# Memory normalised once inside the long plan; GLU and three key blocks as three fp32r products; six key and value blocks traced ahead of the GLU

## The chip, the cores and the metric

The kernel runs on one core of a Trainium2 chip. The metric is the device time of one execution in microseconds. The engines are named as the profile names them: PE is TensorE (matmuls; PEld its weight loads), DVE is VectorE, ACT is ScalarE, POOL is GpSimd, and SP is the engine whose queue issues nearly all transfers (SPq). Each engine works through its instructions in program order.

## The reference

A two-layer encoder trunk on 512 frames of 1024 channels with 256 memory tokens. Layer 0 projects the normalised input once and feeds two branches: an S5 state-space mixer with a GLU, and a convolution module; layer 1 is chunked attention. Each layer then cross-attends to the memory. The parts that the change touches:

```python
def s5_mixer(...):
    ...
    y = y.reshape(bsz, L, S5_WIDTH) + d_skip * uf
    z = jax.nn.gelu(y)
    out = z * jax.nn.sigmoid(z @ glu_w + glu_b)          # GLU: 512 x 512

def mem_cross_attention(h, mem_n, w_qg, w_kv, w_o):
    q, g = jnp.split(h @ w_qg, 2, axis=-1)
    k, v = jnp.split(mem_n @ w_kv, 2, axis=-1)           # 1024 x 2048, in both layers
    ...
    return (o * jax.nn.silu(g)) @ w_o

def reference(...):
    mem_n = rms_norm(mem, mem_norm_g)
    for layer in range(DEPTH):
        x = x + (ssm_conv_layer if layer % 2 == 0 else chunk_attention_layer)(...)
        x = x + mem_cross_attention(rms_norm(x, xa_norm_g[layer]), mem_n, ...)
    return rms_norm(x, final_norm_g)
```

## The kernel before, in words

All activations lie transposed: 128 channels on the partitions, tokens along the free axis, so x is eight tiles of 128x512 and the memory eight of 128x256. A matrix product in float32 is made of three products of rounded operands (type fp32r): each operand is split into a rounded part "hi" and the rest "lo", and hi·hi, hi·lo and lo·hi are added up in PSUM (mm3, proj). A weight block of 512 KB is loaded into one of three buffers "raw", ACT rounds it into "whi" (two buffers), and POOL, or DVE where the call says so, subtracts to get "wlo" (three buffers); this is weights(), and split() does the same for activations. A few products use the float32 operands as they are (native): the GLU's four blocks (line 923), key blocks 0 to 2 of layer 0 (NATIVE, line 704; the branch of line 664), and the S5, convolution and broadcast products.

Layer 0 is one long plan (PLAN, line 705): u, z, c and g are blocks of the input projection, v steps of the convolution's taps (two loads "cw" each), a, b and o the preparation, the scan and the output of one S5 slice of four, m and n the memory's statistics, l and s the LayerNorm of the convolution. m loads the eight memory tiles into two buffers "mt", squares them on ACT and adds them up on POOL; n makes the reciprocal root. After the plan come the GELU of the S5 outputs (zs), the memory's normalisation (mem_norm, line 631), which loads the memory again tile by tile, makes a float32 copy in "uu" and its hi and lo parts in "og", then the four GLU blocks, the LayerNorm's application, and the twelve key and value blocks of layer 0 in the order KVORDER, and the output projection w_out. A key block is 24 matmuls of 256 columns as three products, a value block 48 (token_major). In layer 1 mem_norm (line 1377) loads and normalises the memory a third time.

What the text gives is the traced order. Between the start of the plan and the first cross-attention PE's instructions are not pinned to it: a scheduler sorts each engine's instructions by readiness and priority when the program is built, and code under tc.high_priority() goes first. On the chip the resulting order of each engine is fixed. A buffer of a tag is handed out again when its last reader has finished, so an instruction or a load that writes a new tile may wait for that.

## Time and profile before

| | |
|---|---|
| median of 3 runs | 988.85 us (988.27 to 993.58) |
| profiled execution | 992.0 us, span 990.1 us |
| PE busy | 958.3 us (97%) |
| PEld busy | 820.5 us (83%) |
| DVE, ACT, POOL busy | 561.1, 468.8, 441.3 us |
| DMA | 113.72 MB, mean 115 GB/s |

The span goes from the first to the last instruction of the profiled execution. Busy time of PE is modelled from the starts of the matmuls; a native float32 matmul shows as two records. The granted clock is given as a share of full speed, so 0.50 is 1.2 GHz.

### The profile page before, as it was taken

How to read it: one execution, taken by the hardware profiler on the slowest of the kernel's cores; microseconds unless marked ns; L12 is line 12 of the kernel's file. 1: busy time of each engine (PE TensorE's matmuls, PEld its weight loads, DVE VectorE, ACT ScalarE, POOL GpSimd, SP SyncE). 2: the span in 40 equal slices, each digit the busy share in tenths (PEclk: the TensorE clock that was granted, in tenths of full speed). 3: DMA queues.
4: the chain of work that ended last, by engine and by line, in shares of the span. 5: the costliest groups of instructions: out<-in, count | busy, mean ns of one | idle time of the engine just before them, and what ended most of it. 6: DMA issues, size and time to landing. Idle time of an engine off the chain costs nothing.

```text
span 990.1 us, 14347 instructions
## 1 busy us (share of the span) xinstructions
PE 958.3 (97%) x5336; PEld 820.5 (83%) x5336; DVE 561.1 (57%) x1372; ACT 468.8 (47%) x845; POOL 441.3 (45%) x245
## 2 busy tenths in 40 slices
PE   8999999989999999999999999999999999999996
PEld 7788898858888888888798887877888998888895
DVE  7975356766244334453568767688667313333476
ACT  6333445456443434344366655656545543333352
POOL 1022332129766334447645434444327983433241
PEclk9999997999999999999999999999999999999998
...
GB/s 292 119 194 177 196 160 170 113 127 234 192 85 107 65 85 64 84 75 107 65 96 75 75 67 94 75 75 75 65 43 139 156 185 107 64 86 79 50 169 108
DMA packets 53621, 113.72 MB, mean 115 GB/s; under 512 B 13232, under 2 KB 24624, under 8 KB 53552
## 3 DMA queue, kind: packets, MB, share of 16 engines
...
q8 instruction: 42, 0.69, 0.3%
q14 instruction: 27, 0.22, 0.1%
...
## 4 chain that ended last, share of the span: by engine, by line
PE 33%; DVE 10%; ACT 3%; issue 2%; POOL 1%; DMA 1%; POOLq 0%; DVEq 0%; ACTq 0%
PE ps_proj L81 27%; PE ps_att L81 2%; PE ps_tr L84 2%; DVE pe L158 2%; DVE ps_att L1275 1%; PE ps_acc L81 1%; DVE o L153 1%; ACT whi L173 1%; PE ps_tr L81 1%; DVE h L162 1%; ACT pe L1262 1%; POOL wlo L153 1%; DVE z L153 1%; DVE s L1274 1%; DVE qk L153 1%
## 5 line engine op out<-in xcount | busy, mean ns | idle before, releaser
L153 POOL TENSOR_TENSOR wlo<-raw,whi 128x1024 fp32r<-128x1024 f32 x130 | 317.2, 2444 | 406.6 <-ACT whi L173 360.1
L81 PE MATMUL ps_proj<-h,whi 128*128 128x512 f32 x1184 | 302.0, 399 | 2.4 <-DVE ang L153 2.4
L81 PEld LDWEIGHTS ps_proj<-h,whi 128*128 128x128 f32 x1184 | 218.9, 190 | 47.6 <-issue 5.1
L173 ACT CAST whi<-raw 128x1024 fp32r<-128x1024 f32 x148 | 155.3, 1050 | 197.7 <-PE ps_proj L81 97.2
L81 PE MATMUL ps_proj<-h,wlo 128*128 128x512 f32 x592 | 151.0, 393 | 0.0
L81 PE MATMUL ps_proj<-og,whi 128*128 128x512 f32 (+1 forms) x672 | 134.9, 347 | 0.5 <-DVE og L153 0.5
L81 PEld LDWEIGHTS ps_proj<-h,wlo 128*128 128x128 f32 x592 | 110.8, 189 | 22.6
L81 PEld LDWEIGHTS ps_proj<-og,whi 128*128 128x128 f32 x672 | 107.6, 188 | 18.0 <-DVE og L153 2.0
L81 PE MATMUL ps_proj<-og,wlo 128*128 128x512 f32 (+1 forms) x344 | 73.5, 348 | 0.1
L81 PEld LDWEIGHTS ps_proj<-og,wlo 128*128 128x128 f32 x344 | 56.1, 188 | 8.8 <-POOL wlo L153 0.4
L153 DVE TENSOR_TENSOR pt<-ps_tr,pt 128x512 fp32r<-128x512 f32 (+1 forms) x80 | 40.0, 527 | 34.8 <-ACT pt L173 34.7
L173 ACT CAST pt<-ps_tr 128x512 fp32r<-128x512 f32 (+1 forms) x80 | 34.2, 460 | 48.2 <-PE ps_tr L84 48.0
L1262 ACT ACTIVATE pe<-ps_att,s 128x128 f32<-128x128 f32 (+3 forms) x64 | 33.5, 525 | 37.7 <-DVE s L167 34.0
L158 DVE TENSOR_SCALAR_CACHE_REDUCE pe<-pe,s 128x256 f32<-128x256 f32 (+3 forms) x96 | 48.5, 522 | 1.8
L153 DVE TENSOR_TENSOR z<-ps_proj,rb 128x512 f32<-128x512 f32 x32 | 22.1, 690 | 45.4 <-PE ps_proj L81 45.3
L153 POOL TENSOR_TENSOR sa<-sa,sq 128x512 f32<-128x512 f32 (+1 forms) x28 | 39.0, 1394 | 18.7 <-ACT sq L233 18.3
L153 DVE TENSOR_TENSOR x<-ps_proj,x 128x512 f32<-128x512 f32 (+1 forms) x38 | 22.9, 603 | 41.5 <-PE ps_proj L81 41.5
L153 DVE TENSOR_TENSOR kv<-ps_proj,kv 128x256 fp32r<-128x256 f32 (+1 forms) x24 | 12.2, 510 | 60.2 <-ACT kv L173 59.3
L162 DVE SCALAR_TENSOR_TENSOR h<-x,par,h 128x512 fp32r<-128x512 f32 x24 | 38.5, 1612 | 13.5 <-ACT h L252 13.5
L81 PEld LDWEIGHTS ps_proj<-x,cw 128*128 128x128 f32 x320 | 41.9, 202 | 4.7 <-DMA cw<-in_cw_dram 2.4
L81 PE MATMUL ps_proj<-x,cw 128*128 128x64 f32 (+4 forms) x320 | 41.4, 281 | 2.3 <-DMA cw<-in_cw_dram 1.7
L84 PE MATMUL ps_tr<-ident,pe 128*128 128x128 f32 x224 | 34.2, 274 | 3.4 <-DVE pe L158 2.4
...
## 6 DMA issues: line engine op xcount, KB each, us to landing
...
```

The source lines that it names most:

```text
L81: return self.keep(nc.tensor.matmul(*args, **kw))
L84: return self.keep(nc.tensor.transpose(*args))
L153: (eng or V).tensor_tensor(out, a, b, op=op)
L158: V.tensor_scalar(out=out, in0=in0, scalar1=s, scalar2=None, op0=op, op1=ALU.add, accum_out=small(1))
L162: V.scalar_tensor_tensor(out=out, in0=a, scalar=s, in1=b, op0=op0, op1=op1)
L173: A.copy(hi, src)
L1262: A.activation(st_["pe"][i], ps[:, c:c + n], AF.Exp, bias=nb, accum_out=st_["sums"][:, i:i + 1])
L1274: V.reduce_max(init, ps[:, :nf], axis=AX.X)
L1275: V.tensor_tensor_reduce(out=ps[:, nf:n], in0=ps[:, nf:n], in1=st["tz"][:, MEM - (n - nf):], scale=1.0, scalar=init, op0=ALU.add, op1=ALU. ...
```

## The change

The memory tiles are loaded once for layer 0, in pairs, into the "x" buffers that the plan leaves free, squared from there, kept, and normalised in a new stage w of the plan between a3 and b3; n moves ahead of a3. Their hi parts go to "ev" tiles and their lo parts to one "uu" and three "x" tiles, without a float32 copy. NATIVE and the native branches are gone: the three key blocks and the GLU are three products like the rest, and the GLU's inputs are split on ACT and DVE. In layer 0 the weight splits of the key and value blocks alternate between DVE and POOL. Six of these blocks are traced before the GLU (KVFIRST), the other six stay behind it. Outputs that had "ev" tiles of their own overwrite "sq", "gate" and "uu" tiles. In layer 1 the memory is loaded in four pairs into "kv" buffers.

```diff
@@ -120,7 +120,7 @@
     sm = ctx.enter_context(tc.tile_pool(name="sm", bufs=1))
     pp = ctx.enter_context(tc.tile_pool(name="pp", bufs=1, space=bass.MemoryType.PSUM))
     dr = ctx.enter_context(tc.tile_pool(name="dr", bufs=1, space=bass.MemoryType.DRAM))
-    base = Phase("base", {"raw": 3, "whi": 2, "wlo": 3, "x": 8, "h": 16, "rb": 1, "sq": 2, "sa": 1, "dg": 1, "mt": 2}).open()
+    base = Phase("base", {"raw": 3, "whi": 2, "wlo": 3, "x": 8, "h": 16, "rb": 1, "sq": 2, "sa": 1, "dg": 1}).open()
     ctx.callback(base.close)
 
     PS = {"proj": 3, "att": 2, "tr": 2, "acc": 1}
@@ -182,11 +182,6 @@
         with tc.high_priority():
             split(raw, hi, lo, eng)
         return hi, lo
-
-    def whole(src, kt=8, n=P):
-        raw = tl("raw", (P, kt, n))
-        nc.sync.dma_start(raw, src)
-        return raw
 
     def mm3(ps, terms, cuts=()):
         prods = []
@@ -620,36 +615,31 @@
         nc.sync.dma_start(y, yd.rearrange("q c s j -> (q c) s j"))
         return y
 
-    def mem_load():
-        st = Stats(MEM)
-        for i in range(KT):
-            t = tl("mt", (P, MEM))
-            nc.sync.dma_start(t, memT_d[i])
-            st.add(t, pin=True)
-        return st
-
-    def mem_norm(rs, tag, raw_tag=None):
-        mm, raw = [], []
-        with tc.high_priority():
-            rbm = bcast(rs, MEM)
-            for i in range(KT):
-                t = tl("mt", (P, MEM))
-                nc.sync.dma_start(t, memT_d[i])
-                tt(t, rbm, t, ALU.mult)
-                e = rl(tag, (P, 2, MEM))
-                if raw_tag is None:
-                    mm.append(gsplit(t, pc("mem_g", i), e[:, 0], e[:, 1]))
-                else:
-                    if i % 2 == 0:
-                        m = tl(raw_tag, (P, 2, MEM))
-                    raw.append(m[:, i % 2])
-                    A.activation(raw[i], t, AF.Copy, scale=pc("mem_g", i))
-                    mm.append(split(raw[i], e[:, 0], e[:, 1], V))
-        return mm, raw
-
-    def token_major(outs, act, ws_d, eng=None):
+    def mem_load(tag, st=None):
+        tiles = []
+        for i in range(0, KT, 2):
+            t = tl(tag, (P, 2, MEM))
+            nc.sync.dma_start(t, memT_d[i:i + 2].rearrange("i p s -> p i s"))
+            for e in range(2):
+                if st is not None:
+                    st.add(t[:, e], pin=True)
+                tiles.append(t[:, e])
+        return tiles
+
+    def mem_norm(rs, tiles, his, los):
+
+        mm = []
+        rbm = bcast(rs, MEM)
+        for i, t in enumerate(tiles):
+            tt(t, rbm, t, ALU.mult)
+            if i % 2 == 0:
+                hi, lo = rl(his[i // 2], (P, 2, MEM)), rl(los[i // 2], (P, 2, MEM))
+            mm.append(gsplit(t, pc("mem_g", i), hi[:, i % 2], lo[:, i % 2]))
+        return mm
+
+    def token_major(outs, act, ws_d, eng):
         for e in range(2):
-            wh, wl = weights(ws_d[e], kt=4, n=MEM, eng=eng)
+            wh, wl = weights(ws_d[e], kt=4, n=MEM, eng=eng())
             for low in range(2):
                 for t, o in enumerate(outs):
                     ts_ = slice(t * P, (t + 1) * P)
@@ -659,15 +649,15 @@
                             T.matmul(o, a[:, ts_], b[:, k, :], start=(e == 0 and low == 0 and t % 2 == 0 and k == 0 and j == 0),
                                      stop=(e == 1 and low == 1 and t % 2 == 1 and k == 3))
 
-    def kv_units(layer, mm, raw=None, native=()):
+    def kv_units(layer, mm, engs=(None,)):
+        count = [0]
+
+        def eng():
+            count[0] += 1
+            return engs[count[0] % len(engs)]
+
         def keys(i):
-            if ("k", i) in native:
-                w = whole(xa_k_d[layer, i])
-                ps = psum("proj")
-                for j in range(KT):
-                    T.matmul(ps[:, :MEM], w[:, j, :], raw[j], start=(j == 0), stop=(j == KT - 1))
-            else:
-                ps = proj(weights(xa_k_d[layer, i]), mm, n=MEM)
+            ps = proj(weights(xa_k_d[layer, i], eng=eng()), mm, n=MEM)
             e = rl("kv", (P, 2, MEM))
             with tc.high_priority():
                 split(ps[:, :MEM], e[:, 0], e[:, 1], V)
@@ -676,15 +666,7 @@
         def values(h):
             hi, lo = rl("kv", (P, 2, MEM)), rl("kv", (P, 2, MEM))
             ps = psum("proj")
-            if ("v", h) in native:
-                for e in range(2):
-                    w = whole(xa_v_d[layer, h, e], kt=4, n=MEM)
-                    for t in range(2):
-                        for j in range(4):
-                            T.matmul(ps[:, t * MEM:(t + 1) * MEM], raw[4 * e + j][:, t * P:(t + 1) * P], w[:, j, :],
-                                     start=(e == 0 and t == 0 and j == 0), stop=(e == 1 and t == 1 and j == 3))
-            else:
-                token_major([ps[:, :MEM], ps[:, MEM:]], mm, [xa_v_d[layer, h, e] for e in range(2)])
+            token_major([ps[:, :MEM], ps[:, MEM:]], mm, [xa_v_d[layer, h, e] for e in range(2)], eng)
             with tc.high_priority():
                 split(ps.rearrange("p (m c) -> p m c", m=2), hi, lo, V)
             vv[h] = (hi, lo)
@@ -700,9 +682,9 @@
             run["v"](i)
         return kv
 
-    KVORDER = [('k', 2), ('k', 0), ('k', 1), ('v', 3), ('k', 4), ('v', 0), ('k', 6), ('k', 3), ('k', 5), ('v', 2), ('v', 1), ('k', 7)]
-    NATIVE = [('k', 0), ('k', 1), ('k', 2)]
-    PLAN = "u0 u1 z0 c0 u2 u3 z1 c1 g0 v0 t0 g1 v0 v0 v0 a0 z2 b0 c2 v1 v1 v1 v1 g2 o0 a1 z3 b1 c3 v2 v2 v2 v2 g3 o1 a2 m0 g4 b2 v3 v3 v3 v3 g5 o2 a3 b3 n0 g6 l0 s0 o3 g7"
+    KVFIRST = [('v', 0), ('k', 0), ('k', 1), ('v', 1), ('k', 2), ('k', 3)]
+    KVORDER = [('v', 2), ('k', 4), ('k', 5), ('v', 3), ('k', 6), ('k', 7)]
+    PLAN = "u0 u1 z0 c0 u2 u3 z1 c1 g0 v0 t0 g1 v0 v0 v0 a0 z2 b0 c2 v1 v1 v1 v1 g2 o0 a1 z3 b1 c3 v2 v2 v2 v2 g3 o1 a2 m0 g4 b2 v3 v3 v3 v3 g5 o2 n0 a3 w0 b3 g6 l0 s0 o3 g7"
     UENG = 'VVVVVVVVVVGG'
     GATE_V = (0, 3, 5, 7)
     s5p = Phase("s5", {"l1": 2, "cs": 2, "m": 6, "g": 2, "y": 2, "s16": 48, "s32": 4}, side="right").open()
@@ -871,12 +853,16 @@
     mem = {}
 
     def mem_sums(i):
-        mem["st"] = mem_load()
+        mem["st"] = Stats(MEM)
+        mem["x"] = mem_load("x", mem["st"])
 
     def mem_scale(i):
         T.ordered = True
         mem["rs"] = mem["st"].done()
         T.ordered = False
+
+    def mem_parts(i):
+        mem["mm"] = mem_norm(mem["rs"], mem.pop("x"), ["ev"] * 4, ["uu", "x", "x", "x"])
 
     lst = Stats()
 
@@ -894,7 +880,7 @@
     def ln_scale(_):
         lst.rs = lst.done(1.0 / 512)
 
-    stages = {"u": state_input, "z": conv_gate, "c": conv_input, "a": prep, "b": scan, "o": out, "g": gate, "m": mem_sums, "n": mem_scale, "v": conv_taps,
+    stages = {"u": state_input, "z": conv_gate, "c": conv_input, "a": prep, "b": scan, "o": out, "g": gate, "m": mem_sums, "n": mem_scale, "w": mem_parts, "v": conv_taps,
               "l": ln_centre, "s": ln_scale, "t": tables}
     for job in PLAN.split():
         stages[job[0]](int(job[1:]))
@@ -902,8 +888,8 @@
 
     zs = []
     for sl in range(4):
-        t = tl("uu")
-        stt(t, uP[sl].rearrange("p s j -> p (s j)"), pc("s5_d", sl), ys[sl].rearrange("p s j -> p (s j)"), ALU.mult, ALU.add)
+        t = uP[sl].rearrange("p s j -> p (s j)")
+        stt(t, t, pc("s5_d", sl), ys[sl].rearrange("p s j -> p (s j)"), ALU.mult, ALU.add)
         A.activation(t, t, AF.Gelu_apprx_tanh)
         zs.append(t)
 
@@ -914,33 +900,32 @@
     for i in range(8):
         if gates[i] is None:
             gate(i)
-    mm, mraw = mem_norm(mrs, "og", "uu")
+    run, kv0 = kv_units(0, mem["mm"], (G, V))
+    for kind, i in KVFIRST:
+        run[kind](i)
 
     for g in gates:
         A.activation(g, g, AF.Silu)
+    zp = [split(t, rl("og"), rl("og"), V) for t in zs]
     yg = [None] * 8
     for i in range(4):
-        w = whole(glu_w_d[i], 4)
-        ps = psum("proj")
-        for k in range(4):
-            T.matmul(ps, w[:, k, :], zs[k], start=(k == 0), stop=(k == 3))
-        sg = tl("ev")
+        ps = proj(weights(glu_w_d[i], kt=4, eng=V), zp)
+        sg = tl("sq")
         A.activation(sg, ps, AF.Sigmoid, bias=pc("glu_b", i))
         tt(sg, zs[i], sg, ALU.mult, G)
-        o = tl("ev")
+        o = gates[i]
         tt(o.rearrange("p (j s) -> p j s", s=4), sg.rearrange("p (s j) -> p j s", s=4),
-           gates[i].rearrange("p (j s) -> p j s", s=4), ALU.mult)
+           o.rearrange("p (j s) -> p j s", s=4), ALU.mult)
         yg[i] = split(o, rl("og"), rl("og"))
 
-    run, kv0 = kv_units(0, mm, mraw, NATIVE)
     def ln_apply():
         lb = bcast(lst.rs, SEQ)
         for i in range(4):
             t = tt(conv[i], lb, conv[i], ALU.mult)
             A.activation(t, t, AF.Silu, scale=pc("ln_g", i), bias=pc("ln_b", i))
-            o = tl("ev")
+            o = gates[4 + i]
             tt(o.rearrange("p (j s) -> p j s", s=CP), t.rearrange("p (s j) -> p j s", s=CP),
-               gates[4 + i].rearrange("p (j s) -> p j s", s=CP), ALU.mult)
+               o.rearrange("p (j s) -> p j s", s=CP), ALU.mult)
             yg[4 + i] = split(o, rl("og"), rl("og"), V)
 
     ln_apply()
@@ -1374,7 +1359,8 @@
 
     kvp = Phase("kv1", {"kv": 16}, side="right").open()
     xap = Phase("xa1", XA).open()
-    mm, _ = mem_norm(mrs, "q")
+    with tc.high_priority():
+        mm = mem_norm(mrs, mem_load("kv"), ["q"] * 4, ["q"] * 4)
     residual(od_out_d, og, first=PARTS)
     h, st = norm_split("xa_g", 8)
     kv1 = kv_proj(1, mm)
```

On PE, the end of the last gate block (ps_proj_1961 in before, ps_proj_1990 in after), as it was:

```order
L81 MATMUL ps_proj_1961<-h_154,wlo_1958 128x512
L81 MATMUL ps_proj_1961<-h_156,wlo_1958 128x512
L81 MATMUL ps_proj_1961<-h_158,wlo_1958 128x512
L81 MATMUL ps_proj_2083<-uu_1988,raw_2081 128x512
L81 MATMUL ps_proj_2083<-uu_1991,raw_2081 128x512
L81 MATMUL ps_proj_2083<-uu_1994,raw_2081 128x512
```

And the same place now; whi_2038 is a value weight, ev and uu_1800 are memory tiles:

```order
L81 MATMUL ps_proj_1990<-h_154,wlo_1987 128x512
L81 MATMUL ps_proj_1990<-h_156,wlo_1987 128x512
L81 MATMUL ps_proj_1990<-h_158,wlo_1987 128x512
L81 MATMUL ps_proj_2035<-whi_2038,ev_1799 128x256
L81 MATMUL ps_att_1962<-uu_453,M 128x128
L81 MATMUL ps_proj_2035<-whi_2038,uu_1800 128x256
L81 MATMUL ps_proj_2035<-whi_2038,ev_1799 128x256
```

Native GLU products (uu with raw) followed the gate; now the first value block does, with one S5 output product among its matmuls.

On PE, the S5 output of scan 3 (ps_att; hh is the state that the scan leaves), which stood inside the last gate block:

```order
L81 MATMUL ps_proj_1961<-h_152,whi_1957 128x512
L81 MATMUL ps_att_1933<-hh_109,w_101 128x128
L81 MATMUL ps_proj_1961<-h_153,whi_1957 128x512
L81 MATMUL ps_proj_1961<-h_154,whi_1957 128x512
L81 MATMUL ps_att_1933<-hh_110,w_102 128x128
```

And now, inside key block 0 (whi_2100):

```order
L81 MATMUL ps_proj_2104<-x_1824,whi_2100 128x256
L81 MATMUL ps_att_1962<-hh_109,w_101 128x128
L81 MATMUL ps_proj_2104<-ev_1799,wlo_2101 128x256 x2
L81 MATMUL ps_proj_2104<-ev_1807,wlo_2101 128x256
L81 MATMUL ps_att_1962<-hh_110,w_102 128x128
L81 MATMUL ps_att_1962<-uu_453,M 128x128
```

The scan's products moved from the last gate block to two blocks later.

On SP, the loads around the first conv weights of slice 3 (cw_1633 in before, cw_1625 in after; names in brackets are what an instruction waits for), as it was:

```order
L830 DMA cd_1415<-x_1078 128x8x64 [waits DMAHW7_49,Activation_49]
L627 DMA mt_1524<-in_memT_dram 128x256 [waits DMAHW0_49]
L620 DMA y_1473<-yd_1468 128x512 [waits DMAHW5_49,DMAHW4_49,DMAHW6_49,DMAHW3_49,DMAHW1_49]
L627 DMA mt_1529<-in_memT_dram 128x256 [waits DMAHW2_49]
L832 DMA x_1417<-cd_1415 128x512 [waits DMAHW7_49]
L821 DMA cw_1633<-in_cw_dram 128x640 [waits PE_49]
L627 DMA mt_1534<-in_memT_dram 128x256 [waits DMAHW0_49,Activation_49]
L627 DMA mt_1539<-in_memT_dram 128x256 [waits DMAHW2_49,Activation_49]
L821 DMA cw_1640<-in_cw_dram 128x640 [waits PE_49]
```

And now:

```order
L812 DMA cd_1415<-x_1078 128x8x64 [waits Activation_49]
L803 DMA cw_1625<-in_cw_dram 128x640 [waits DMAHW5_49,DMAHW4_49,PE_49]
L615 DMA y_1473<-yd_1468 128x512 [waits DMAHW2_49,DMAHW7_49,DMAHW1_49,DMAHW0_49]
L814 DMA x_1417<-cd_1415 128x512 [waits DMAHW6_49,DMAHW3_49]
L622 DMA x_1505<-in_memT_dram 128x2x256
L622 DMA x_1512<-in_memT_dram 128x2x256
L622 DMA x_1520<-in_memT_dram 128x2x256
L622 DMA x_1528<-in_memT_dram 128x2x256 [waits PE_49]
L803 DMA cw_1632<-in_cw_dram 128x640
```

The first conv load moved ahead of the loads of y and x, and the memory loads stand together and wait for no ACT instruction.

On DVE, scan 3 began with its products in one piece; now the memory's normalisation stands behind the first of them:

```order
L153 TENSOR_TENSOR m_1865<-ps_att_1830,cs_1785 128x512
L153 TENSOR_TENSOR x_1505<-ps_acc_1796,x_1505 128x256 x2
L153 TENSOR_TENSOR x_1512<-ps_acc_1796,x_1512 128x256
L162 SCALAR_TENSOR_TENSOR uu_1800<-x_1505,par,ev_1799 128x256 x2
L153 TENSOR_TENSOR x_1512<-ps_acc_1796,x_1512 128x256
L162 SCALAR_TENSOR_TENSOR x_1808<-x_1512,par,ev_1807 128x256
L153 TENSOR_TENSOR x_1520<-ps_acc_1796,x_1520 128x256 x2
L153 TENSOR_TENSOR x_1528<-ps_acc_1796,x_1528 128x256
L153 TENSOR_TENSOR wlo_2039<-raw_2036,whi_2038 128x1024
L153 TENSOR_TENSOR gate_1916<-ps_proj_1891,rb_380 128x512
```

The products m_1866 and on, the scan itself and hh come behind these and the rest of the memory's tiles.

## Rows read from the trace of the kernel before

**Rows 1.** The page's table of engines: busy us (share of the span) xinstructions.

```profile
span 990.1 us, 14347 instructions
...
PE 958.3 (97%) x5336; PEld 820.5 (83%) x5336; DVE 561.1 (57%) x1372; ACT 468.8 (47%) x845; POOL 441.3 (45%) x245
```

**Rows 2.** Weight loads by line and operation: busy us, mean ns, then idle before.

```profile
L81 PEld LDWEIGHTS ps_proj<-og,wlo 128*128 128x128 f32 x344 | 56.1, 188 | 8.8 <-POOL wlo L153 0.4
```

**Rows 3.** PE's timeline, 196 to 311 us: start, duration, instructions, [wait before].

```profile
196.57 5.31 PE L81 MATMUL ps_proj<-uu,raw 128*128 128x512 f32 x12
...
209.60 5.40 PE L81 MATMUL ps_proj<-uu,raw 128*128 128x512 f32 x16 [1.24 <-DMA raw<-in_glu_w_dram]
216.68 3.72 PE L81 MATMUL ps_proj<-uu,raw 128*128 128x256 f32 x16 [1.69 <-ACT uu L646]
...
221.10 5.34 PE L81 MATMUL ps_proj<-uu,raw 128*128 128x256 f32 x24
226.96 2.10 PE L81 MATMUL ps_proj<-whi,og 128*128 128x256 f32 x16 [0.52 <-ACT whi L173]
230.53 1.21 PE L81 MATMUL ps_proj<-wlo,og 128*128 128x256 f32 x8 [1.47 <-POOL wlo L153]
...
246.21 1.98 PE L81 MATMUL ps_proj<-og,whi 128*128 128x256 f32 x16
...
248.93 1.98 PE L81 MATMUL ps_proj<-og,whi 128*128 128x256 f32 x16
...
308.35 1.99 PE L81 MATMUL ps_proj<-og,whi 128*128 128x512 f32 x8
...
311.10 3.96 PE L81 MATMUL ps_proj<-h,whi 128*128 128x512 f32 x16
```

**Rows 4.** PE's wait at 154 us; then windows: busy times, granted clock, DMA share.

```profile
154.92 2.19 PE L81 MATMUL ps_proj<-x,cw 128*128 128x64 f32 x10 [0.68 <-DVE m L153]
...
154.00:156.00 2.00, 1.32 (x9) 1.24 (x9) 2.00 (x5) 1.78 (x5) 0.63 (x2) 0.78 0.85 294
158.00:160.00 2.00, 2.00 (x6) 1.53 (x5) 2.00 (x3) 0.03 (x1) 0.00 (x0) 0.50 0.79 227
164.00:166.00 2.00, 2.00 (x13) 1.90 (x12) 0.00 (x0) 0.00 (x0) 0.00 (x0) 0.66 0.17 67
178.00:180.00 2.00, 2.00 (x20) 1.99 (x19) 0.76 (x2) 0.61 (x2) 0.93 (x2) 1.00 0.42 85
```

**Rows 5.** SP's timeline at 150 us: start, duration with waits between, load.

```profile
150.12 0.43 SPq L821 DMA_DIRECT2D cw<-in_cw_dram  x1
150.81 2.00 SPq L627 DMA_DIRECT2D mt<-in_memT_dram  x2
```

**Rows 6.** DVE: scan 3's two ends (15 instructions); memory tiles, min/median/max ns; weight splits.

```profile
178.95 0.69 DVE L153 TENSOR_TENSOR m<-ps_att,cs 128x512 f32<-128x512 f32 x1 [4.97 <-PE ps_att L81]
...
188.81 1.28 DVE L153 TENSOR_TENSOR hh<-m,m 128x508 f32<-128x508 f32 x2
...
L153 DVE TENSOR_TENSOR mt<-ps_acc,mt x16: 409/425/427, 204.1 to 765.2; 128x256 f32<-128x256 f32 x16
...
L162 DVE SCALAR_TENSOR_TENSOR q<-mt,par,q x8: 469/510/2029, 746.5 to 766.2; 128x256 fp32r<-128x256 f32 x8
...
L153 DVE TENSOR_TENSOR wlo<-raw,whi 128x1024 fp32r<-128x1024 f32 x18 | 22.8, 1268 | 22.7 <-ACT whi L173 16.9 <-issue 5.2 <-PE ps_att L81 0.5
```

**Rows 7.** POOL's and DVE's timelines, pieces that the bounds use.

```profile
175.86 3.12 POOL L153 TENSOR_TENSOR w<-g,g 64x256 f32<-64x256 f32 x4 [18.12 <-PE ps_att L81]
...
227.35 21.89 POOL L153 TENSOR_TENSOR wlo<-raw,whi 128x1024 fp32r<-128x1024 f32 x8
...
229.11 8.37 DVE L153 TENSOR_TENSOR ev<-x,gate 128x512 f32<-128x512 f32 x3 [0.15 <-ACT x L940]
```

**Rows 8.** Layer 1: PE's wait in the key blocks, and SP's memory loads.

```profile
777.80 1.22 PE L81 MATMUL ps_proj<-q,wlo 128*128 128x256 f32 x8 [0.92 <-POOL wlo L153]
...
757.94 5.60 SPq L637 DMA_DIRECT2D mt<-in_memT_dram  x3
```

## The prediction

> **What bounds the kernel now.** I read the page's table of engines first. TensorE is busy for 958.3 of 990.1 us [rows 1], so the time changes by three things only: matmul time added or taken away, waits of TensorE, and its clock. The page's strip of granted clock and a table by windows come next, then TensorE's timeline around the code that changes, and last the queues that it waits for there.
>
> The stretch in question runs from about 150 us (last part of the long plan) to 311 us, where the next stage starts on fully fed 512-column matmuls. In it TensorE is never idle for long, but it stands four times between 209 and 231 us: 1.24 us for a GLU weight load, 1.69 us for the first raw memory tile, 0.52 and 1.47 us for the first split value block [rows 3]. Before that, at 154 us, it waits 0.68 us, and right behind it the granted clock stands at 0.50, that is 1.2 instead of 2.4 GHz, until about 165 us [rows 4].
>
> **The profiled execution and the runs.** The profiled one took 992.0 us, 1.9 more than its span; the median of the three runs is 988.85, and the highest 993.58. The slow stretch in the profile is worth, by the windows' rows, 2 x (0.22 + 4 x 0.50 + 0.34) = 5.1 us (0.78, four rows of 0.50, 0.66) [rows 4]. That is more than the 3.1 us between profile and median, so the median run may be one without it. The sum is made against 992.0 and carried to the median below.
>
> **Part 1: three fp32r products in place of native fp32.** A native product shows as two records. GLU: 16 products, 32 records of 512 columns; twelve take 5.31 us, 0.4425 each [rows 3], so 14.2 us. Key blocks 0 to 2: 24 products, 48 records of 256 columns at 5.34/24 = 0.2225, so 10.7 us. In their place stand 48 fp32r matmuls of 512 columns and 72 of 256. The pace of the first is (311.10 - 308.35)/12 = 0.229, of the second (248.93 - 246.21)/24 = 0.113 [rows 3]: 11.0 and 8.2 us. TensorE gains 3.2 + 2.5 = **5.7 us**. Bound from the other side: at 0.131 per 256 columns (2.10 us for 16 [rows 3]) the keys take 9.4 and the gain is 4.5.
>
> Here a page bears. The Trainium skill, Perfetto Trace Analysis, Identifying the Most-Contended Engine, says that matmul busy time misleads and that the share of weight loads tells how near TensorE is to its limit. The change adds 40 loads; if loads of 0.188 us each [rows 2] set the pace, the three keys would take 72 x 0.188 = 13.5 us, and the change would lose 2.8 us there instead of gaining 2.5. The trace does not agree: the 256-column matmuls step at 0.113 us, faster than one load lasts, so loads overlap one another.
>
> What the splits cost beside it: seven more roundings of weights on ScalarE and twelve more subtractions on VectorE (eight at 1.27 us [rows 6], four of half the size), five fewer on GpSimd. ScalarE and VectorE are busy for 47% and 57% [rows 1], so nothing is charged but the queue order on VectorE, in part 3.
>
> **Part 2: the waits at 209 to 231 us.** All four have one reason: only GLU and raw-memory products stood there, each on a fresh load or a fresh rounding. Now the six key and value blocks stand there, 21.8 us of TensorE work (two values at 48 x 0.113, four keys at 24 x 0.113), whose memory tiles were normalised earlier and whose first weight loads stand in the queue among the conv loads; the GLU's own inputs and loads have that much more time. I take all four away: **-4.9 us**. Bound: none goes if the weight splits are late, a rival below.
>
> **Part 3: the new wait.** The normalisation (eight multiplies at 0.425, eight fused subtractions at 0.510 [rows 6]) now stands on VectorE behind the first product of scan 3 and ahead of the others, with two weight splits (1.27 each). The chain from that first product to the last write of the scan's states took 178.95 to 190.09, 11.1 us, in before, one gate included [rows 6]; now it is 11.1 + 3.4 + 4.1 + 2.5 + 0.7 (a second gate) = 21.8 us. TensorE in the same time: the broadcast and the small products of scan 3 (some 2.4 us), 16 + 24 gate matmuls (9.2), one value block (5.4), two thirds of a key block (1.8): 18.8. It then stands inside key block 0 before the state's first product, with the rest of that block and of all blocks behind it: **+3.0 us**. From below 0 (the memory work may fall into VectorE's own waits); from above 3.0 + 8.6, if it is also held up by every GpSimd operation of this time (3.12 us of table products, two weight splits at 21.89/8 = 2.74 [rows 7]). I take 3.0, nearest to uncontended rows.
>
> **Part 4: the load queue at 150 us.** The wait at 154.24 is put down to VectorE, but the instruction waits for a load too: its conv weights were issued at 150.12, 4.8 us before it ran, behind the loads of y, x and two memory tiles, and the next two memory loads held the queue for 2.00 us [rows 5]. In the new order this load precedes y and x, some 2 us earlier, and the memory loads (four, of twice the size, into free x buffers) have no wait for a squared tile. So the wait of 0.7 goes, and with it, I think, the fall of the clock. What else is queued behind the four loads are the next two conv loads, which TensorE now wants 4 us later. **-0.7 and -5.1 us**, the second uncertain: the same small products without a wait ran at full clock at 178 us [rows 4].
>
> **Part 5: layer 1.** TensorE waited 0.92 us at 777 us for a split that came late, after the memory loads, which waited for their two buffers, had held the queue for 5.60 us ahead of key weights [rows 8]. Now four loads go out together, once the attention stage has left the buffers. Between 0 and -0.9; I take **-0.5**.
>
> **Sum.** 992.0 - 5.7 - 4.9 + 3.0 - 0.5 = 983.9 with the slow stretch, 978.1 without it and its wait. From the median: 988.85 - 8.1 = 980.8 if that run had no slow stretch, 975.0 if it had. I forecast **979.0 us**, its own range 975 to 982.
>
> **Rivals.**
> *The clock falls once more.* The new wait stands between small products, as the one at 154 us did; one stretch like that costs 5.1: 984. For it: the only fall inside this stretch came behind a wait of that kind. Against: at 209 and 216 us longer waits left the clock at full.
>
> *The weight splits set the pace of the six blocks.* Half of them are now on VectorE, in line behind the scan. If each block waits as the first one did in before (1.47 us [rows 3]), that is 8.8 us: 988, no change. For it: GpSimd alone needs 2.74 per split against 2.72 of matmul per key block. Against: two engines share them now, and three load buffers are filled long ahead.
>
> *Slower: VectorE's chain ahead of scan 3.* The fused subtractions of the memory last up to 2.029 us where they meet GpSimd [rows 6]; three VectorE products beside back-to-back GpSimd splits took 8.37 us [rows 7]. If all eight go at 2.03 the chain is 12.2 us longer, TensorE waits 15 us inside key block 0, the clock falls behind it: 979.0 + 12.2 + 5.1 = 996. It decides once that wait passes about 8 us with a fall of the clock, 13 without. Against: by the program's order GpSimd has only some 8.6 us of work in these 22. A page gives the mechanism: by the Trainium skill, SBUF — State Buffer, Who interferes with whom, a VectorE operation with two SBUF inputs and a GpSimd one that reads SBUF shut each other out for a whole instruction; the 8.37 us agree.
>
> *The blocks are not in front in the end* (a scheduler sets the order): excluded, the order shows them between the last gate and the GLU.
>
> **Chances.** Forecast 0.55. The clock falls again 0.20. Splits set the pace 0.10. Better (median with the slow stretch, none after, no new wait; about 974) 0.10. Slower 0.05. About 0.5%, 4.9 us, is what a measurement here can tell from no change, so faster means below 983.9: 0.55 + 0.10 + half of the second case + a little of the third = 0.77; same 0.18; slower 0.05. The range to hold 8 in 10 leaves out the slower case, most of the split case and the best end: 974 to 986.
>
> **What would show it.** Right: no native records but those of S5, conv and broadcasts; TensorE without waits over 1 us from the last gate to the output projection, except one before the first state product, 1 to 4 us inside key block 0; full clock at 150 to 165; the next stage's start some 13 us earlier than 311. Wrong: waits for weight splits in each block; a wait of 8 us or more at the state product; a clock of 0.50 anywhere from 150 to 300 us.

## The result, and the profile after

The changed kernel takes 998.76 us (median of 13 runs, 993.78 to 1003.12) against 988.27 for the kernel before in the same session (983.84 to 993.58), and the ratio of the runs is 1.0087, 95% interval 1.0063 to 1.0111 (that of the two medians alone would be 1.0106). The forecast was 979.0 us, a gain, so both the size and the sign failed.

Each run comes with its span and its mean granted clock, and the product of the two separates two things. In 29 runs of the kernel before, the spans go from 981.6 to 992.9 us, while span times clock stays within 976.2 to 979.3 (median 977.7): what differs from run to run is how long the clock stood at its lower level. Below, "work and waits" is span times clock, and "clock loss" is the rest of the span. For the changed kernel the medians are 980.3 and 17.9 us, for the kernel before 977.7 and 9.9. So the change costs 2.6 us in work and waits and 8.0 us in clock. Both readings are coarse: the clock is given to three places, one of which is 1 us of span, and a wait that falls into a stretch of low clock counts there in part as clock loss (some 2.7 us in the profiled run below).

The table of engines of the changed kernel answers to [rows 1]; VectorE has 22 us more to do, GpSimd 10 less:

```profile
span 997.2 us, 14411 instructions
...
PE 959.4 (96%) x5376; PEld 828.8 (83%) x5376; DVE 583.1 (58%) x1388; ACT 470.0 (47%) x846; POOL 431.1 (43%) x240
```

TensorE's waits of over 0.3 us from 155 us on, from its timeline (start, duration, matmuls, wait before and what ended it), where [rows 3] had four others:

```profile
164.28 0.49 PE L81 MATMUL ps_att<-uu,M 128*128 128x128 f32 x2 [0.88 <-ACT M L575]
...
178.66 0.67 PE L81 MATMUL ps_acc<-dg,ones 128*128 128x256 f32 x2 [0.90 <-DVE dg L167]
...
202.03 0.79 PE L81 MATMUL ps_att<-hh,w 128*128 128x128 f32 x2 [3.68 <-DVE hh L153]
...
215.13 1.05 PE L81 MATMUL ps_acc<-ones,sa 128*128 128x1 f32 x8 [1.32 <-DVE sa L153]
...
249.57 0.58 PE L81 MATMUL ps_proj<-ev,whi 128*128 128x256 f32 x1 [3.96 <-ACT whi L173]
255.73 2.08 PE L81 MATMUL ps_proj<-ev,wlo 128*128 128x256 f32 x8 [2.38 <-DVE wlo L153]
```

The four old waits are gone. The wait of 3.68 us is part 3 of the prediction. The other five stand in no part of it: two short ones in the long plan (the second for the memory's broadcast), with the clock at 1.00 behind them; one for the layer norm's statistics; and two in key block 4 behind the GLU. The windows (us; busy time of PE, PEld, DVE, ACT and POOL, granted clock, DMA share, GB/s) show what follows the longer ones:

```profile
198.00:202.00 4.00, 0.35 (x3) 0.15 (x2) 4.00 (x5) 2.33 (x2) 1.62 (x1) 0.79 0.58 221
202.00:209.00 7.00, 6.97 (x34) 5.94 (x35) 5.48 (x9) 2.41 (x5) 0.00 (x0) 0.63 0.24 91
...
215.00:222.00 7.00, 6.87 (x45) 6.87 (x46) 3.49 (x15) 1.40 (x2) 0.37 (x1) 0.76 0.34 115
...
239.00:248.00 9.00, 6.61 (x50) 5.94 (x48) 4.97 (x4) 3.72 (x6) 7.40 (x5) 1.00 0.34 117
248.00:262.00 14.00, 10.05 (x46) 9.76 (x47) 13.53 (x14) 9.46 (x14) 4.40 (x3) 0.51 0.40 132
```

Behind the waits TensorE runs at 0.51 to 0.76 of its clock. By its busy time that costs 6.97 x 0.37 + 6.87 x 0.24 + 10.05 x 0.49 = 9.2 us; the 3.95 us for which it stands in the last of these windows are counted in the waits already. The next stage starts at 318.64 us, 7.5 later than in [rows 3]; from there to the end it is 678.6 us, before 679.0. In these two executions the whole loss lies in this stretch.

Why key block 4 comes late is seen on ScalarE, whose order is fixed, and on VectorE and GpSimd, which it waits for there:

```profile
238.96 1.04 ACT L173 CAST whi<-raw 128x1024 fp32r<-128x1024 f32 x1
245.25 0.62 ACT L173 CAST og<-gate 128x512 fp32r<-128x512 f32 x1 [5.25 <-DVE gate L153]
245.77 0.68 ACT L914 ACTIVATE sq<-ps_proj,par 128x512 f32<-128x512 f32 x1
246.47 1.28 ACT L925 ACT_TABLE_LOAD   x1
247.77 0.81 ACT L925 ACTIVATE x<-x,par 128x512 f32<-128x512 f32 x1
248.49 1.03 ACT L173 CAST whi<-raw 128x1024 fp32r<-128x1024 f32 x1
```

```profile
242.01 3.20 DVE L153 TENSOR_TENSOR gate<-sq,gate 128x512 f32<-128x512 f32 x1 [2.44 <-POOL sq L153]
```

```profile
240.68 1.30 POOL L153 TENSOR_TENSOR sq<-uu,sq 128x512 f32<-128x512 f32 x1
241.93 2.41 POOL L153 TENSOR_TENSOR wlo<-raw,whi 128x1024 fp32r<-128x1024 f32 x1
```

The rounding of key block 4's weights (248.49) stands behind the rounding of a gated GLU tile; between them are the GLU's last sigmoid, a table load and the layer norm's first activation (245.77 to 248.49). The rounding of the gated tile waits 5.25 us for VectorE's gate product, which waits for GpSimd's and then takes 3.20 us, where one without GpSimd beside it takes 1.06 (at 248.47): GpSimd's split of 2.41 us lies across it.

### The profile page after: what moved, and what is told of

It is laid out like the page before. It is cut to its first block, busy times and chain, and to the rows that moved or that the text cites. A ratio compares the mean times of both kernels' runs of the same rounds, so it can differ in the third digit from the quotient of the medians.

```text
span 997.2 us, 14411 instructions
## 1 busy us (share of the span) xinstructions
PE 959.4 (96%) x5376; PEld 828.8 (83%) x5376; DVE 583.1 (58%) x1388; ACT 470.0 (47%) x846; POOL 431.1 (43%) x240
## 5 line engine op out<-in xcount | busy, mean ns | idle before, releaser
L153 POOL TENSOR_TENSOR wlo<-raw,whi 128x1024 fp32r<-128x1024 f32 x125 | 302.0, 2418 | 457.5 <-ACT whi L173 397.7
L173 ACT CAST whi<-raw 128x1024 fp32r<-128x1024 f32 (+1 forms) x155 | 160.7, 1037 | 203.3 <-PE ps_proj L81 105.8
L81 PEld LDWEIGHTS ps_proj<-og,whi 128*128 128x128 f32 x624 | 104.5, 188 | 18.5 <-DVE og L153 0.6
L153 DVE TENSOR_TENSOR wlo<-raw,whi 128x1024 fp32r<-128x1024 f32 (+1 forms) x30 | 38.7, 1290 | 24.6 <-ACT whi L173 23.3
L153 POOL TENSOR_TENSOR sa<-sa,sq 128x512 f32<-128x512 f32 (+1 forms) x28 | 43.0, 1537 | 7.2 <-ACT sq L228 6.5
L81 PEld LDWEIGHTS ps_proj<-x,cw 128*128 128x128 f32 x320 | 39.1, 192 | 3.4 <-DMA cw<-in_cw_dram 2.3
L81 PE MATMUL ps_proj<-x,cw 128*128 128x64 f32 (+4 forms) x320 | 39.2, 271 | 1.0 <-DMA cw<-in_cw_dram 1.0
```

The source lines that it names most:

```text
L81: return self.keep(nc.tensor.matmul(*args, **kw))
L153: (eng or V).tensor_tensor(out, a, b, op=op)
L173: A.copy(hi, src)
```

## The experiments

Each kernel has 4 to 13 runs. Times are us; ratios are to the kernel before on the same chip; "waits" is the sum of TensorE's from 140 to 312 us in the profiled run (6.1 in the kernel before), which is one execution. Chips differ (the kernel before has medians of 988.2 to 989.7 on them), so kernels are compared by their ratios; with intervals of 0.0025 to either side, which most have, two ratios have to differ by about 0.0035, or 3.5 us, to be told apart.

| kernel | median | ratio, 95% | work and waits | clock loss | waits |
|---|---|---|---|---|---|
| changed | 998.8 | 1.0087 [1.0063, 1.0111] | 980.3 | 17.9 | 13.4 |
| two_loops | 995.9 | 1.0074 [1.0048, 1.0100] | 980.1 | 13.9 | 13.5 |
| w_early2 | 993.6 | 1.0045 [1.0020, 1.0070] | 977.6 | 14.9 | 11.5 |
| native_glu | 995.7 | 1.0073 [1.0041, 1.0104] | 981.4 | 13.9 | 10.8 |
| all_front | 996.9 | 1.0079 [1.0051, 1.0108] | 980.4 | 14.9 | 13.6 |
| p1_alone | 1001.7 | 1.0135 [1.0090, 1.0179] | 980.7 | 20.0 | 14.4 |
| g_only | 1000.9 | 1.0135 [1.0098, 1.0171] | 984.2 | 15.0 | 18.1 |
| native_k45 | 994.6 | 1.0074 [1.0047, 1.0100] | 979.4 | 12.9 | 11.4 |
| w2_native_k45 | 993.1 | 1.0039 [1.0018, 1.0060] | 979.8 | 11.4 | 10.4 |
| undo_p1 | 992.1 | 1.0041 [1.0016, 1.0066] | 981.8 | 8.4 | 8.8 |
| mem_alone | 994.5 | 1.0072 [1.0048, 1.0096] | 983.5 | 10.9 | 8.2 |
| w2_undo_p1 | 996.8 | 1.0084 [1.0044, 1.0123] | 983.4 | 11.4 | 11.3 |
| fill_wait | 999.7 | 1.0108 [1.0071, 1.0146] | 980.4 | 17.0 | 11.7 |
| layout | 997.6 | 1.0090 [1.0058, 1.0123] | 980.9 | 15.9 | 14.4 |
| ln_later | 993.7 | 1.0046 [1.0023, 1.0069] | 979.7 | 11.9 | 11.7 |
| undo_lay_ln | 991.6 | 1.0028 [1.0001, 1.0055] | 980.8 | 8.9 | 8.9 |
| w2_ln_s | 988.7 | 1.0001 [0.9975, 1.0028] | 975.7 | 10.8 | 9.2 |
| w3_ln_s | 987.4 | 0.9997 [0.9966, 1.0028] | 976.4 | 9.4 | 8.3 |
| w3_ln_late | 988.9 | 1.0008 [0.9986, 1.0031] | 977.4 | 8.9 | 8.6 |

**Part 1 alone** (p1_alone), on the kernel before:

```
-    NATIVE = [('k', 0), ('k', 1), ('k', 2)]
+    NATIVE = []
...
-    mm, mraw = mem_norm(mrs, "og", "uu")
+    mm, mraw = mem_norm(mrs, "og")
...
+    zp = [split(t, rl("h"), rl("h"), V) for t in zs]
...
+        ps = proj(weights(glu_w_d[i], kt=4, eng=V), zp)
```

> The kernel before with part 1 alone: the GLU and key blocks 0 to 2 as three fp32r products; the memory is loaded twice and normalised behind the plan, and all twelve blocks stand behind the GLU, as before. Two readings are used from here on: the time itself, and span times mean granted clock, which takes out the falls of the clock (29 runs of the kernel before: 976.2 to 979.3, median 977.7, where the spans run from 981.6 to 992.9). Theory of the prediction (each product costs its pace): -5.7 us in span times clock, 972, and about 984 in time. Theory D (the native blocks were cover: they need no rounded weights and no split memory, so TensorE had 24.9 us of work right there while ScalarE, VectorE and GpSimd finished the memory and the GLU's last steps): new waits of 4 us or more stand at the first key block behind the GLU, span times clock is 976 or more, and the clock falls behind them: 989 to 996.

It is 13.5 us slower than the kernel before (four runs; 8.9 to 17.7 by the interval). TensorE's waits there (engine, tile, line, what it waited for: total us, times, longest):

```profile
PE ps_proj L81 <- ACT og L252: 5.8, 1, 5.8
PE ps_proj L81 <- DVE h L153: 3.6, 2, 2.2
PE ps_proj L81 <- POOL wlo L153: 2.1, 2, 1.3
PE ps_proj L81 <- ACT h L173: 2.0, 2, 1.5
```

The GLU waits 5.6 us for the splits of its inputs, the first key block 5.8 for the rounded memory. Waits grow by 14.4 - 6.1 = 8.3 us, work and waits by only 3.0. Some of that gap comes from waits at low clock, which count there in part; the rest is matmul time saved, and more than was saved was given back as waits. The clock takes the rest (windows: us, PE busy, granted clock, DMA share, GB/s):

```profile
190.00:200.00 10.00, 7.38 (x28) 0.82 0.39 108
200.00:210.00 10.00, 7.02 (x17) 0.50 0.28 92
210.00:220.00 10.00, 7.06 (x39) 1.00 0.36 131
220.00:230.00 10.00, 6.83 (x22) 0.51 0.30 92
```

The waits of theory D are there, with a time above its 989 to 996: native products were cover. They want a load and no split, so TensorE had work there while the other engines finished.

**The other parts without part 1** (undo_p1): native GLU, and for key blocks 0 to 2

```
+            if i in native:
+                w = tl("raw", (P, KT, P))
...
+                    T.matmul(ps[:, :MEM], w[:, j, :], raw[j], start=(j == 0), stop=(j == KT - 1))
```

> The changed kernel with part 1 undone in full: GLU native, key blocks 0 to 2 native on a float copy of the normalised memory; the memory in the long plan, its single load, the blocks in front of the GLU and their splits on two engines stay. By the paces alone +5.7 us on the changed kernel in span times clock: 980.3 + 5.7 = 986, and a time of 1003. Theory D (native products are cover, part 1 loses by the waits it lays open; part 1 alone on the kernel before cost 13.5 us in time, 3.0 of it in span times clock): 975 to 980 in span times clock, 986 to 994 in time, the wait for key block 4's rounding gone. Between the two: key blocks 0 to 2 stand in front of the GLU here, where the wait is for scan 3's state and a native block covers nothing: then only the GLU's share comes back, as in the run with the GLU alone (995.7).

By the ratios it is 4.5 us below the changed kernel (6.7 by the medians). Its longest wait in this stretch is 1.95 us (scan 3's state; then 1.8 for a rounding behind the GLU), and in the same kind of windows the clock does not fall once, in what was the fastest of its ten runs (clock loss 5.9, median 8.4):

```profile
190.00:200.00 10.00, 8.05 (x59) 1.00 0.32 102
...
220.00:230.00 10.00, 10.00 (x31) 1.00 0.22 68
...
240.00:250.00 10.00, 8.44 (x64) 1.00 0.37 122
250.00:260.00 10.00, 8.08 (x64) 1.00 0.69 233
```

Work and waits are above the forecast for theory D and 1.5 over the changed kernel's: the matmul time came back, the waits went only in part. The gain is in the clock, 8.4 against 17.9. It is still 3.4 us over the kernel before, with waits of 8.8 us against 6.1, so parts 2 to 5 lose by themselves.

**Which part of part 1: the GLU, or blocks behind it** (native_glu; native_k45 with key blocks 4 and 5 native)

> Leaves out nothing; the GLU alone is native fp32 again, as in the kernel before, all else as changed (its four weight splits, and the splits of the four S5 tiles, go from ScalarE and VectorE). By the paces alone the GLU takes 14.2 instead of 11.0 us of TensorE: +3.2. Theory A (ScalarE's queue behind the GLU): the GLU's products last longer, so the queue behind them has more time; 998.8 + 3.2 less at most 3 of the waits: 998 to 1002. Theory C (the extra splits of the GLU crowd VectorE and ScalarE): the waits of 3.96, 2.38 and 1.32 us and their half clock go, 998.8 + 3.2 - 7.7 - 8.6 = about 986. Theory B: +3.2, 1002.

> The changed kernel with key blocks 4 and 5, the second and third block behind the GLU, as native fp32 products on raw weights and a float copy of the normalised memory (8 short ScalarE instructions more, two weight roundings and two splits fewer). TensorE has 16 native products there, 32 records x 0.2225 = 7.1 us, where 48 x 0.12 = 5.8 stood: +1.3 by the paces. Theory D (native blocks are cover: they want nothing but a load): the waits of 3.96 and 2.38 us behind the GLU go and the half clock from 248 to 262 with them; span times clock 980.3 + 1.3 - 6.3 = 975, time 988 or less. Theory B or C (the loss is at scan 3, or spread): +1.3, 999 to 1001.

Neither is told apart from the changed kernel (1.0073 and 1.0074 against 1.0087), and neither gives what its theory asked. With the GLU native the wait for ScalarE's rounding falls from 4.0 to 0.4 us, but one of 3.0 for wlo stays. With the two blocks native, no wait for a rounding is left, but one of 3.2 us stands right behind them for the split of a finished value block, which has to leave PSUM and stands behind the gate products on VectorE as well; the wait for scan 3's state is 4.4 us here. So no single prerequisite is the cause; what the traces show each time is the order in VectorE's and ScalarE's queues.

**The order behind the GLU** (two_loops, ln_later, all_front, g_only)

```
+    for i, sg in enumerate(sgs):      # two_loops: gate products and splits in a loop of their own
...
+    for kind, i in KVORDER[:3]:       # ln_later: three blocks ahead of ln_apply()
+        run[kind](i)
+    ln_apply()
...
+run, kv0 = kv_units(0, mem["mm"])     # g_only, in place of (G, V)
```

> Leaves out nothing; only the GLU's last steps are in another order: first the four products, sigmoids and GpSimd's multiplications (the result now written over the S5 tile), then in a second loop the four gate products and their splits. So ScalarE's four sigmoids no longer stand behind the roundings of the gated tiles, and the rounding of key block 4's weights behind both comes earlier. Theory A (the loss behind the GLU comes from ScalarE's queue: the rounding of key block 4's weights stands behind roundings that wait for VectorE and GpSimd): the waits of 3.96 us at 249.57 and 2.38 us at 255.73 go or fall below 1 us each, and with them the half clock from 248 to 262, worth 14 x 0.49 = 6.9 us; 998.8 - 6.3 - 6.9 = about 986. Theory B (the wait for scan 3's state and the clock behind it are the loss): no change from the changed kernel, 996 to 1001. Theory C (the extra splits on VectorE are the loss, whatever their order): no change either, 996 to 1001.

> The changed kernel with the layer norm's last steps (broadcast, eight VectorE products, four activations, four splits) traced behind the first three blocks that follow the GLU, not ahead of them. Theory F (the wait behind the GLU is a matter of order: key block 4's rounding and split stand in ScalarE's and VectorE's queues behind the GLU's and the layer norm's steps): the waits of 3.96 and 2.38 us go, and the half clock from 248 to 262 with them; span times clock 980.3 - 6.3 = 974, time 986 to 990. Rival (those steps have to be done in any case before the output projection, and the six blocks of 21.8 us are too short a cover for them): waits of 3 to 6 us come up at the fifth to eighth unit's products of the output projection, or at the blocks behind, and the time is 992 to 998.

> Leaves out nothing; all twelve key and value blocks of layer 0 stand in front of the GLU, none behind it. Theory A (weights of the blocks behind the GLU wait in ScalarE's queue for the GLU's last steps): the waits of 3.96 and 2.38 us and the half clock from 248 to 262 go (13.2 us), but now the output projection stands right behind the GLU and waits for the GLU's last split: in the changed kernel that is GpSimd's at 250.25 to 251.54, 12.8 us after the GLU's last matmul at 238.72; the broadcast of the layer norm takes 0.5 and the chain loses its collisions with the blocks' weight splits (some 4 us), so a wait of 6 to 12 us comes in, with a clock that may fall behind it: 991 to 1000. Theory B (the state's wait is the loss): that wait stays, and the time is 996 or more.

> The changed kernel with every weight split of the twelve blocks on GpSimd, none on VectorE. Theory E (the blocks' splits on VectorE are the loss: they stand in its queue behind the GLU's gate products and the layer norm's, and the state of scan 3 behind two of them): the wait of 2.38 us for wlo goes, and the wait for scan 3's state falls by 1.3 to 2.5 us; with the clock about 992. Rival (GpSimd becomes the bound: 2.4 us a split against 2.88 of matmul per key block, and the GLU's four products and four splits besides): waits for GpSimd's wlo come in their place, 998 or more. Theory D: the wait for key block 4's rounding (3.96 us, ScalarE) stays, since it does not come from the splits.

In two_loops the rounding comes nearly in time (wait 0.3 us), and the split on VectorE is now what ends a wait of 5.8 us: the same total, so theory A, which put the loss in ScalarE's queue alone, fell. ln_later takes 4.1 us off by the ratios (5.1 by the medians); 1.8 us are left for the rounding, and 2.1 come in for inputs of the output projection (its rival, in part). With all blocks in front, the waits move to the output projection, 1.4 and 4.5 us where 6 to 12 were expected. With all splits on GpSimd the wait of 2.4 us for wlo goes, as theory E asked, but the state of scan 3 comes 6.6 us late instead of 3.7: VectorE then meets more of GpSimd's splits, and its four products ahead of the state take 6.74 us there, 4.66 in the changed kernel. The rounding of key block 4 still comes 4.0 us late. So theory E fell: the splits on VectorE were not too many, both engines together are short of time here.

**The place of the memory's normalisation** (w_early2; w2_native_k45; mem_alone and w2_undo_p1 with part 1 undone)

```
-... o0 a1 z3 b1 c3 v2 v2 v2 v2 g3 o1 a2 m0 g4 b2 v3 v3 v3 v3 g5 o2 n0 a3 w0 b3 g6 ...
+... o0 a1 z3 b1 c3 m0 v2 v2 v2 v2 g3 o1 a2 n0 w0 g4 b2 v3 v3 v3 v3 g5 o2 a3 b3 g6 ...
```

> Leaves out nothing; in the long plan the memory's loads are placed after the convolution input of slice 3, and its sums and normalisation before the gate job 4, so before scan 2 instead of beside scan 3. Theory B (the memory's normalisation on VectorE ahead of scan 3's state is the loss): TensorE's wait of 3.68 us at 202.03 goes, and the granted clock of 0.63 from 202 to 209 (7 x 0.37 = 2.6 us) with it; 998.8 - 3.7 - 2.6 = about 992.5, and 990 if the 1.32 us wait and the 0.76 at 215 to 222 go too. Theory A (the loss is behind the GLU): the same 3.7 go, but the waits of 4.0 and 2.4 us behind the GLU and their half clock stay in the trace. A third way: the normalisation now delays scan 2 and the wait turns up there, no change, 997 to 1001.

> The kernel before's blocks and products (GLU and key blocks 0 to 2 native, all twelve blocks behind the GLU in the old order, splits on GpSimd) with the memory alone changed: loaded once and normalised inside the long plan, at the early place that took 2 us off the wait for scan 3's state. Theory D: this takes away the kernel before's waits of 1.69, 0.52 and 1.47 us (for the first raw memory tile and the first split value block) and brings no new one: span times clock 977.7 - 3.7 = 974, time 980 to 985, below the kernel before. Rival (the memory's normalisation costs in the plan what it saves behind it, since VectorE is late for the S5 states already): 977 to 980 and 988 to 992.

> Key blocks 4 and 5 native as in the run with them alone, and the memory's loads and normalisation earlier in the long plan, as in the run with that alone (which took 993.55 and had its wait for scan 3's state cut from 3.7 to 1.7 us). If the two losses add up (theory D behind the GLU, theory B at scan 3): span times clock about 975 - 2.7 = 972, time 980 to 985, below the kernel before. If one wait only moves to the other place: 988 to 994.

> Part 1 undone in full and the memory at the early place of the plan; six blocks in front of the GLU as changed. Against the run with part 1 undone alone it shows what the memory's place is worth; against the run with the memory alone, what the six blocks in front of the GLU do. Theory D: span times clock 2 to 3 us below the run with part 1 undone, 974 to 978, time 982 to 990. Rival (the blocks in front bring scan 3's state a wait in either place, since their matmuls are short of its chain): a wait of 1.7 to 4 us stays at the state with half clock behind it, 990 to 995.

On the changed kernel the early place takes 4.2 us off by the ratios (5.2 by the medians); the wait for the state falls from 3.7 to 1.7, and one of 1.5 us for the memory's broadcast comes in at 150 us. Without part 1 it does not help: in mem_alone TensorE reaches the GLU before the last GELU and waits 4.3 us there, and w2_undo_p1 is 4.7 us over undo_p1 on the same chip. With key blocks 4 and 5 native the state's wait is even 4.9. These gains do not add up. The order on each engine is sorted anew for every edit, and a wait turns up at another place.

**Two that settled less** (fill_wait, layout)

```
+                for j in range(NFILL):                      # fill_wait, 16 products ahead of key block 0
+                    T.matmul(pf, h0[j % 8][0][:, :P], h0[j % 8][0], ...)
...
+            e = rl((his + los)[i], (P, 2, MEM))             # layout
+            mm.append(gsplit(t, pc("mem_g", i), e[:, 0], e[:, 1]))
```

> The changed kernel with 16 useless fp32r matmuls of 512 columns on old gate tiles set ahead of key block 0, nine of them before scan 3's first state product: 16 x 0.229 = 3.7 us more TensorE work, nine of them (2.1 us) inside the wait of 3.68 us. Theory B2 (the clock falls because TensorE stands still there, and what follows pays for it): the stretch from 200 to 209 runs at full clock, 2.6 to 3.4 us come back, and the time changes by 3.7 - 2.1 - 3 = -1.4, 996 to 999. Rival (the clock falls because of the small products themselves, wait or no wait): it stays at 0.5 to 0.6 there, and the kernel is 1.6 us or more slower, 1000 to 1003.

> The changed kernel with one thing put back as in the kernel before: the high and the low half of a normalised memory tile stand side by side in one buffer, where the change puts the high halves of two tiles in one buffer and their low halves in another. Theory G (the pace of the blocks' 256-column products depends on it: 2.88 us per 24 in the changed kernel, 2.72 to 2.83 in the kernel before): the pace goes back and 384 products save 0.002 to 0.007 each, 1 to 2.7 us; span times clock 977.6 to 979.3. Rival (the pace has another reason, such as the traffic beside it): 2.88 per 24 stays and the time is that of the changed kernel, 996 to 1001.

The fillers did not fill the wait: the sorting put nine of them where the first 16 products of key block 0 had stood and moved those behind it, the wait stayed at 3.5 us, and nothing follows for the clock. In layout 24 products of 256 columns take 2.88 us as in the changed kernel, so theory G is refuted. Its premise was half a reading: the kernel before's thirteen blocks of 24, from 226.96 to 265.79 us, take from 2.72 to over 3 us each, and TensorE is busy for 37.25 us in them, 2.87 a block. Why the pace varies from block to block stays open.

**Mended versions** (undo_lay_ln; w2_ln_s: w_early2, ln_later, and the layer norm's statistics behind the GLU; w3_ln_s: n0 and w0 later; w3_ln_late: statistics behind two blocks)

> Parts 2 to 5 of the change without part 1 (GLU and key blocks 0 to 2 native), with the memory's halves side by side and the layer norm's last steps behind the first three blocks that follow the GLU. That run without the two mends took 992.1 (span times clock 981.8), with waits of 1.95, 1.77 and 0.51 us. If theories F and G hold: 981.8 less 1 to 2.7 for the pace and 2.3 for the waits behind the GLU, 977 to 978.5 in span times clock, and with its 8.4 us of clock loss a time of 986 to 989, level with the kernel before or just below. If neither holds: 990 to 994.

> The changed kernel with three mends: the memory loaded and normalised early in the long plan (alone -5.2 us), the layer norm's last steps behind the first three blocks that follow the GLU (alone -5.1 us), and the layer norm's statistics product moved from between the key blocks to behind the GLU, which takes its wait of 1.32 us and the clock of 0.74 to 0.92 from 215 to 225 (1.7 us) out of the front blocks. If the causes add up: 998.8 - 5.2 - 5.1 - 2 = 986.5, just below the kernel before, with span times clock 980.3 - 2.7 - 0.6 - 1.3 = 975 to 976. If they share a part (the clock that falls once for two waits, or a wait that turns up at the next place): 989 to 992, level with the kernel before.

> As the run before it, with the memory's sums behind gate job 4 and its normalisation inside the last conv taps, behind scan 2 in place of ahead of it: the wait of 1.5 us for the memory's broadcast at 145 should go (its small chain has gate products beside it), and the one for scan 3's state should stay at 1.7 us or less. 1 to 3 us below the run before it if so, 984 to 986; if the normalisation meets scan 3 again, the state's wait is back at 3 us or more and the time is 990 to 993.

> As the last run, with the layer norm's statistics (one product and a chain of eight VectorE operations on four columns) behind the second block after the GLU in place of right behind the GLU. There it ran beside GpSimd's splits, 2.12, 1.20 and 1.22 us for operations that last 0.16 alone, ahead of key block 4's split on VectorE. If that chain is what is left: the wait of 3.35 us falls below 1.5 and the half clock at 241 to 249 (3.5 us) goes; 987.4 - 2 - 3.5 = 982, below the kernel before by 0.6%. If the GLU's own chain (sigmoid, GpSimd's product, VectorE's gate) holds the split up as well: a wait of 2 to 3 us stays and the time is 986 to 988. If the layer norm is now late for the output projection: a wait there, 988 to 991.

undo_lay_ln, without part 1, gains nothing clear on undo_p1 (1.0028 against 1.0041): neither of its theories holds there. With the order behind the GLU and the memory's place mended, the three products come level with the kernel before: w2_ln_s is at 1.0001, 8.5 us below the changed kernel by the ratios; its work and waits (975.7) were as worked out, its time (988.7) lies between its two cases. The two w3 kernels are not told apart from it, and none beats the kernel before beyond its interval. In w3_ln_s the wait at 145 us is gone and one of 3.3 us is left behind the GLU, with half clock behind it; on VectorE, ahead of the split that ends it, three small operations each last until a GpSimd operation ends:

```profile
233.51 0.14 DVE L169 TENSOR_SCALAR s<-ps_acc 128x4 f32<-128x4 f32 x1
233.69 2.12 DVE L169 TENSOR_SCALAR s<-s 128x4 int32<-128x4 int32 x1
235.84 1.20 DVE L153 TENSOR_TENSOR s<-s 128x4 f32<-128x4 f32 x1
237.08 1.22 DVE L153 TENSOR_TENSOR s<-s,s 128x4 f32<-128x4 f32 x1
238.33 0.16 DVE L162 SCALAR_TENSOR_TENSOR s<-s 128x4 f32<-128x4 f32 x1
```

```profile
232.68 3.10 POOL L153 TENSOR_TENSOR wlo<-raw,whi 128x1024 fp32r<-128x1024 f32 x1
235.74 1.29 POOL L153 TENSOR_TENSOR og<-gate,og 128x512 fp32r<-128x512 f32 x1
236.98 1.29 POOL L153 TENSOR_TENSOR sq<-uu,sq 128x512 f32<-128x512 f32 x1
```

Moved away from there (w3_ln_late), the same chain takes 0.15 to 0.17 us an operation:

```profile
243.66 0.15 DVE L169 TENSOR_SCALAR s<-s 128x4 int32<-128x4 int32 x1
```

Still 2.0 and 1.6 us of waits stay in that place, for splits behind the GLU's own chain, as in the middle one of its three cases, and waits of 1.0 and 1.2 us stand at the output projection; the time, 988.9, is that of the third.

## Why the prediction was wrong, point by point

- **Part 1, -5.7: the step that failed.** "Nothing is charged but the queue order on VectorE", because ScalarE and VectorE are busy for 47% and 57%, was wrong. Those are shares of the whole span; from 248 to 262 us VectorE is busy for 13.5 of 14 us. The list of splits is short as well: it leaves out those of the four S5 tiles, which the GLU as three products needs (VectorE has 16 instructions more, not 12), and in p1_alone the GLU waits 5.6 us for just these. The matmul time was nearly right: products of 512 columns step at 0.23 us, which saves 3.2 in the GLU, and those of 256 columns at 0.120 rather than 0.113 (the mean of the kernel before was 0.119, the forecast read its fastest blocks), which saves 2.1 in the keys. By itself part 1 costs 13.5 us, on top of the others 4.5 by the ratios.
- **Part 2, -4.9.** The four waits went. The prediction took all six blocks in front as cover for the GLU and did not ask what then covered the GLU's last steps and the next blocks' roundings. In the kernel before three native key blocks stood there; now 4.0 and 2.4 us of waits do. The second rival came true in part: rounding and split were late, but in one block, not in each.
- **Part 3, +3.0.** 3.7 us measured, at the place named; the chain on VectorE took 24.1 us (178.44 to 202.57) where 21.8 were worked out:

```profile
178.44 0.68 DVE L153 TENSOR_TENSOR m<-ps_att,cs 128x512 f32<-128x512 f32 x1
...
201.30 1.27 DVE L153 TENSOR_TENSOR hh<-m,m 128x508 f32<-128x508 f32 x2
```

- **The clock, put at nothing in the sum.** The first rival had it, once, at 5.1 us and with a chance of 0.20. It came true at three places, 9.2 us. In the two profiled executions forecast (978.1, without the slow stretch) and measured time (998.95) are 20.9 us apart: waits of 13.4 us where the sum leaves 6.1 - 4.9 - 0.7 + 3.0 = 3.5 make 9.9, the clock 9.2, the pace of the three key blocks 0.5; some 1.3 stay open.
- **Part 4, -0.7 and -5.1.** The conv wait is gone, the first block starts at 190.30 us (the GLU at 196.57 in [rows 3]), and the clock is 1.00 from 150 to 160. But p1_alone, with the loads in the old order (its conv weights are issued at 150.20 us, behind the loads of y and x), has neither the wait nor the fall: the same product starts at 154.34 without a wait, and the clock is 1.00 up to 190 us. So the load order is not shown to be the reason for either, and that both were gone was luck. Ten us later the changed kernel has the new wait of 0.88 us.
- **Part 5, -0.5.** From the next stage to the end 0.4 us less: right in size, not in its reason. The memory loads no longer stand among those of the key weights, and the wait that was named is still 0.83 us for 0.92; one of 0.36 us (773.76 in the kernel before) is gone. Ahead of the split that ends it GpSimd goes from split to sum to split without a pause:

```profile
784.60 1.22 PE L81 MATMUL ps_proj<-q,wlo 128*128 128x256 f32 x8 [0.83 <-POOL wlo L153]
```

```profile
778.09 2.40 POOL L153 TENSOR_TENSOR wlo<-raw,whi 128x1024 fp32r<-128x1024 f32 x1
780.46 1.75 POOL L153 TENSOR_TENSOR sa<-sa,sq 128x512 f32<-128x512 f32 x1
782.16 7.10 POOL L153 TENSOR_TENSOR wlo<-raw,whi 128x1024 fp32r<-128x1024 f32 x3
```

- **The slower rival** named the right engines (VectorE's chain met by GpSimd's splits; 3.20 against 1.06 us for one gate product), but their main loss lies behind the GLU, not ahead of scan 3.
- The page rule weighed in part 1 (Trainium skill, Perfetto Trace Analysis, Identifying the Most-Contended Engine) would have put the loss in weight loads. No run shows that: the blocks' products step at 0.120 us wherever no wait stands and the clock is full, faster than a load of 0.188 [rows 2].
